# Split input weights kept in device memory for the later blocks, and another placing of the first Fourier transfers, in a hybrid encoder layer

## The chip, the cores and the metric

The kernel runs on one core of one Trainium2 chip. The metric is the device time of one execution in microseconds (us): the median of three runs of the kernel before is 3038.52 us (3036.92 to 3041.12). The engines are named as in the profile: PE multiplies matrices, with PEld for its weight loads; DVE works on vectors, ACT does activations, casts and copies, POOL does general vector work, and SP issues most of the DMA transfers. A transfer is issued by an engine in the order of that engine's program.

## The reference

One encoder layer over two sequences, 1024 tokens (prompt) and 2048 tokens (sample), model width 1024. Shortened:

```python
u = rms_norm(h, norm_w)
proj = u @ w_in
z_f, u_f, z_s, xbc, dt_raw = split(proj)
# Fourier group: 8 groups of 64 channels
four = fft2(u_f, axes=(seq, channel), norm='ortho').real
y_f = einsum(four, w_fmix) * silu(z_f)
# bidirectional state-space group: 24 heads of 64, 4 groups, state 128, chunks of 128
xbc = silu(conv5(xbc) + conv_b);  xs, Bm, Cm = split(xbc)
dt_f, dt_b = softplus(dt_raw + bias)
y_s = ssd_chunked(xs, dt_f, A_f, Bm, Cm) + flip(ssd_chunked(flip(xs), ...)) + D * xs
y_s = group_rms_norm(y_s * silu(z_s)) * ssd_norm_w
h = h + concat(y_f, y_s) @ w_out
h = h + (p @ w_ple_in) * sigmoid(h @ w_ple_gate)
out = rms_norm(h, final_norm_w)
```

Everything is float32. The matrix products keep nearly that precision by splitting each factor into a high part (the value rounded to the matmul's fp32r format) and a low part (the rest), with three products: high by high, high by low and low by high.

## The kernel before

**Stage 1** (0 to about 1977 us in the profile) does the normalization, the input projection and the whole state-space group. It runs over three blocks of about 1024 tokens: the prompt (block 0) and the two halves of the sample (blocks 1 and 2). The normalized rows of a block stay on the chip, transposed, as `uh` and `ul`, in three pieces of 342 tokens. The projection is cut into 40 *jobs* of 128 output columns each (C, B, x and z for the state-space group, uf and zf for the Fourier group) and a small one for dt. A job has three *pieces*, one for each 342 tokens: 24 matmuls into `ps` (L361), then a copy or a gate out of PSUM.

The weights of a job, 1024 by 128 values, come straight from `w_in` into the one buffer `wr` (`weights_in`, L179 to L183, issued by SP in L182). `weights_split` (L185 to L191) makes two tiles from them: ACT casts `wh<-wr` (L189), and POOL subtracts, `wl<-wr,wh` (L190). There are two buffers each of `wh` and `wl`. Each of the three blocks loads and splits all 40 jobs anew, which makes 120 of each.

Stage 1 has an order written out by hand. One slot is one piece, and `pre(slot, ...)` and `post(slot, ...)` put other work ahead of it or behind it; `step()` (L286) emits what is due. The list `rows_` (L729 to L743) names the jobs in their order: a first row with C, dt and B taken in turns piece by piece; uf 0; then x and z of each of the 12 units (a pair of heads), with the other jobs between; a last row with uf 3 and zf 3 in turns. The weights' times are set in L746 to L758:

```python
j.split_at = max(coming[m - 2].last + 1, k.split_at + 2)
pre(k.split_at + 1, j.load)
pre(j.split_at, j.split)
```

For a job in the steady rows this places the split three slots ahead of the job's first matmul, and the load two slots ahead of the split.

In the slots of each unit stands the state-space work: broadcast rows come back from device memory (`R<-ROWd` L540, `er<-EXPd` L635), POOL masks them (L548), ACT takes exponentials (L558), DVE joins them, PE multiplies (`pd` L575). POOL makes the weighted inputs `xw` (L587), from which PE makes the chunk states `pst` (L607); POOL also applies the gates (L658 to L663), and SP stores y (`Yd<-y`, L667). Of dt, `dt_turned`, `dt_softplus`, `dt_sums` (PE's `pcs` L469, then `acs` on ACT, L471) and `dt_rows` (PE's `prw`, L493) follow the first row at slots that are written down in L806 to L817. In the last row of a block the next block's x is loaded, normalized and turned (`x_in`, `x_norm`, `x_turn`; PE's `pt` L264, then `uh` L267 and `ul` L268). The conv's four outer taps are on DVE (L402).

**Stage 2** (about 1977 to 2101 us) is the Fourier group of both sequences, first the prompt's. It needs the block matrices `bd` and `wbd`, the stored projections U and the tables `traw`, all requested by SP (L900, L907, L913, L928). PE's first product here is `pm<-wbd,bd` (L972), and DVE folds U (`Ue<-U`, L982). **Stage 3** (to about 2700 us) is the output projection, in a scheme of seven products for a pair of chunks (L1102), and **stage 4** does the gated embedding and the final norm. In stages 2 to 4 a scheduler sets the order. Pools of SBUF grow from a left and a right side, so that a tile of a new stage can start when the tile that had its place is no longer read.

Of the kernel before, what the change touches and what calls it, by code (L numbers as in the profile page):

```python
# [18 lines left out]
P = 128  # L19
# [37 lines left out]
def tile_hybrid_encoder(ctx: ExitStack, tc: tile.TileContext, a):  # L57
# [20 lines left out]
    WSd = [dram.tile([P, 7, 4, 512], F32, name=f"WSd{i}") for i in range(3)]  # L78
    PLd = dram.tile([P, 2, DM], F32, name="PLd")
# [22 lines left out]
    with ExitStack() as ph:  # L102
# [76 lines left out]
        def weights_in(c0):  # L179

            raw = wp.tile([P, KT, P], F32, tag="wr", bufs=1, name="wr")
            nc.sync.dma_start(raw, w_in[:, c0:c0 + P].rearrange("(k p) c -> p k c", p=P))  # L182
            return raw  # L183

        def weights_split(raw):  # L185

            wh = wp.tile([P, KT, P], F32R, tag="wh", name="wh")
            wl = wp.tile([P, KT, P], F32R, tag="wl", name="wl")
            S.copy(wh, raw)  # L189
            G.tensor_tensor(wl, raw, wh.bitcast(F32), op=ALU.subtract)  # L190
            return wh, wl  # L191

# [43 lines left out]
        U = {}  # L236

# [74 lines left out]
        class Job:  # L312
# [64 lines left out]
            def end(self):  # L377
                B, k, i, s_ = self.B, self.kind, self.i, slot[0]
                if k == "C":
                    B.CT[i] = CT = gp.tile([P, TB], F32, tag="CT", name="CT")  # L380
                    conv(16 + i, self.dst, CT, s_ + (2 if i else 4))
# [348 lines left out]
        for bi, B in enumerate(blocks):  # L730
# [3 lines left out]
            rows_.append((B, [J("dt"), J("C"), J("B")] if bi else [J("C"), J("dt"), J("B")], "first"))  # L734
# [10 lines left out]

        n_, coming = 0, []  # L746
        for _, js, _ in rows_:
            for k, j in enumerate(js):
                j.last = n_ + 2 * len(js) + k
                if j.c0 is not None:  # L750
                    coming.append(j)
            n_ += 3 * len(js)
        coming[0].split_at = coming[1].split_at = -1
        for m in range(2, len(coming)):
            j, k = coming[m], coming[m - 1]
# [19 lines left out]
        with tc.manual_schedule():  # L775
# [23 lines left out]
            for i in range(3, 9):  # L799
                if i > 3:  # L800
                    pre(i - 4, x_norm, b0, i)
                if i > 5:
                    pre(i - 6, x_in, b0, i)
                post(i - 3, x_turn, b0, i)
# [76 lines left out]
    with ExitStack() as ph:  # L881
# [51 lines left out]
        for i in range(2):  # L933
            load_table(i, (0, 1))
# [451 lines left out]
```

## Time and profile before

| | us |
|---|---|
| median of three runs | 3038.52 |
| the profiled execution | 3031.59 |
| its span | 3029.8 |
| stage 1 | 0 to about 1977 |
| stage 2, Fourier group | 1977 to 2101 |
| stage 3, products | 2101 to 2700 |
| stage 4, outputs | 2700 to 3030 |

The profiled execution is 6.93 us under the median. The page gives for each engine the time in which it was busy; the windows give the same for a stretch of the span, with the granted clock of PE, the mean busy share of the DMA engines and the rate that they moved. A line of the waits reads "engine and its instruction <- who ended the wait: us in total, times, longest". A line of the timeline reads "start, duration, engine, line, operation, output<-inputs", with the idle time just before it and its releaser in brackets. A row with SPq is SP's DMA queue: the time it took to issue, waits included.

Two places of the profile outside the prediction's rows: in stage 3 PE is busy for 509.34 of 549.00 us (2101 to 2650), and in stage 4 for 320.97 of 329.80 us.

### The profile page before, as it was taken

The page shows a single profiled execution, that of the slowest core. Times are in us where ns is not written, and L with a number is a line of the kernel's source. Part 1 is how long each engine was busy: PE and PEld are TensorE (multiplying, and loading weights), DVE is VectorE, ACT ScalarE, POOL GpSimd, SP SyncE. Part 2 cuts the span into 40 slices and gives each one's busy share as a digit, 9 for nine tenths or more (in the row PEclk, how much of TensorE's full clock was granted, in tenths as well). Part 3 has the DMA queues.
Part 4 walks back from the last instruction along what each step waited for, and adds up shares of the span by engine and source line. Part 5 has one row for each costly group of instructions (what it writes and reads, how often), then busy time and mean ns, then how long its engine had stood idle before and what let it go on. Part 6 is the DMA issues. An engine that isn't in the chain of part 4 may idle for free. (4 is left out here: it accounts for less than half of the span.)

```text
span 3029.8 us, 47051 instructions
## 1 busy us (share of the span) xinstructions
PE 2836.0 (94%) x17252; PEld 2566.2 (85%) x17252; DVE 2228.9 (74%) x3412; ACT 1389.1 (46%) x2980; POOL 1475.5 (49%) x1114
## 2 busy tenths in 40 slices
PE   6899999989999899989999999969999899989998
PEld 6899989988999889989999999957677677768887
DVE  3687767666687568666779787687989988875665
ACT  4444545434544454434544444434433533354554
POOL 1355645431567565642555655455777578610000
PEclk9999999999999999999999999979999999999999
DMA  3378878972588778862677787566554644352221
GB/s 96 76 129 162 158 157 173 139 142 79 125 171 167 152 181 165 154 167 64 127 154 146 159 144 158 117 210 250 173 184 132 236 149 150 133 198 91 94 85 69
DMA packets 454579, 440.56 MB, mean 145 GB/s; under 512 B 24384, under 2 KB 405444, under 8 KB 450508
## 3 DMA queue, kind: packets, MB, share of 16 engines
q1 hardware_dynamic: 454060, 436.50, 60.6%
q8 instruction: 137, 2.24, 0.3%
q14 instruction: 94, 0.77, 0.1%
q10 hardware_dynamic: 288, 1.05, 0.1%
HBM read 328.41 MB, written 110.10 MB: 145 GB/s over the span
## 5 line engine op out<-in xcount | busy, mean ns | idle before, releaser
L361 PE MATMUL ps<-uh,wh 128*128 128x342 f32 (+1 forms) x2880 | 961.6, 334 | 8.4 <-ACT uh L267 8.4
L361 PE MATMUL ps<-ul,wh 128*128 128x342 f32 (+1 forms) x2880 | 926.3, 322 | 2.5 <-DVE ul L268 2.5
L361 PE MATMUL ps<-uh,wl 128*128 128x342 f32 (+1 forms) x2880 | 927.4, 322 | 0.4 <-POOL wl L190 0.4
L190 POOL TENSOR_TENSOR wl<-wr,wh 128x1024 fp32r<-128x1024 f32 x120 | 305.5, 2546 | 707.9 <-ACT wh L189 650.5
L361 PEld LDWEIGHTS ps<-uh,wh 128*128 128x128 f32 x2880 | 552.2, 192 | 20.1 <-ACT uh L267 9.2
L361 PEld LDWEIGHTS ps<-ul,wh 128*128 128x128 f32 x2880 | 554.5, 193 | 4.2 <-DVE ul L268 3.5
L361 PEld LDWEIGHTS ps<-uh,wl 128*128 128x128 f32 x2880 | 550.4, 191 | 1.2 <-POOL wl L190 1.1
L558 ACT ACTIVATE R<-R,lb 128x128 f32<-128x128 f32 x1152 | 356.8, 391 | 98.3 <-POOL R L548 98.2
L548 POOL TENSOR_SCALAR_AFFINE_SELECT R<-R 128x512 f32<-128x512 f32 x288 | 257.5, 905 | 193.7 <-DMA R<-ROWd 187.2
L618 DVE SCALAR_TENSOR_TENSOR H<-H,cd,pst 128x64 f32<-128x64 f32 x888 | 182.6, 274 | 47.7 <-PE pst L607 44.6
L402 DVE SCALAR_TENSOR_TENSOR xT<-raw,cvt,xT 128x1024 f32<-128x1024 f32 x144 | 214.8, 1492 | 2.6
L1102 PE MATMUL X<-whP,ah 128*128 128x512 f32 x480 | 195.2, 407 | 8.0 <-ACT pu L1111 6.4
L1102 PE MATMUL X<-wlP,ah 128*128 128x512 f32 x480 | 193.6, 403 | 1.6 <-DVE wlP L861 1.6
L1102 PE MATMUL X<-whP,al 128*128 128x512 f32 x480 | 192.5, 401 | 2.4 <-DVE al L1073 2.4
L587 POOL TENSOR_TENSOR xw<-xm,wd 128x512 f32<-128x512 f32 x144 | 181.8, 1268 | 18.7 <-PE pst L607 18.5
L367 ACT COPY raw<-ps 128x342 f32<-128x342 f32 x180 | 78.3, 438 | 241.7 <-PE ps L361 226.8
L1214 POOL TENSOR_TENSOR ht<-ht,pu 128x512 f32<-128x512 f32 x96 | 151.9, 1590 | 63.1 <-ACT pu L1111 43.0
L607 PE MATMUL pst<-xw,Bm 128*128 128x128 f32 x1056 | 151.3, 285 | 24.0 <-POOL xw L587 23.8
L607 PEld LDWEIGHTS pst<-xw,Bm 128*128 128x128 f32 x1056 | 131.9, 192 | 41.6 <-POOL xw L587 30.3
L189 ACT CAST wh<-wr 128x1024 fp32r<-128x1024 f32 x120 | 125.8, 1049 | 67.9 <-DMA wr<-in_w_in 67.2
L1073 DVE TENSOR_TENSOR al<-s,ah 128x512 fp32r<-128x512 f32 x144 | 143.6, 1021 | 16.4 <-ACT ah L1072 16.3
L563 DVE TENSOR_TENSOR R<-R,R 128x512 f32<-128x512 f32 x144 | 134.1, 931 | 25.9 <-ACT R L558 23.5
(264 smaller groups left out, 5703.9 us busy)
## 6 DMA issues: line engine op xcount, KB each, us to landing
R<-ROWd SPq DMA_DIRECT2D x288, 256.0 KB
wr<-in_w_in SPq DMA_DIRECT2D x120, 512.0 KB
er<-EXPd SPq DMA_DIRECT2D x288, 128.0 KB
Hd<-ht SPq DMA_DIRECT2D x48, 512.0 KB
ht<-Hd SPq DMA_DIRECT2D x48, 512.0 KB
y<-Yd SPq DMA_DIRECT2D x46, 512.0 KB
wlP<-WSd SPq DMA_DIRECT2D x21, 1024.0 KB
Yd<-y SPq DMA_DIRECT2D x72, 256.0 KB
```

The source lines that it names most:

```text
L190: G.tensor_tensor(wl, raw, wh.bitcast(F32), op=ALU.subtract)
L361: T.matmul(ps[:, :n], lhsT=wt[:, kt, :], rhs=ut[:, kt, :n], start=(i == 0), stop=(i == 3 * KT - 1))
L402: V.scalar_tensor_tensor(dst, raw[:, k:k + TB], cvt[:, 20 * k + ct:20 * k + ct + 1], dst, op0=ALU.mult, op1=ALU.add)
L548: G.affine_select(out=R.rearrange("p c h l -> p (c h) l"), in_=R.rearrange("p c h l -> p (c h) l"), pattern=[[0, 4], [sgn, P]], compare_op ...
L558: S.activation(R[:, c, h, :], R[:, c, h, :], AF.Exp, bias=self.B.lb[:, 2 * p + c, hc + h:hc + h + 1])
L563: V.tensor_tensor(E[0], E[0], E[1], op=ALU.add)
L587: G.tensor_tensor(xw, self.xm[c4].rearrange("p c (h e) -> p c h e", h=2), col(self.B.wd[:, c4:c4 + 4, hc:hc + 2]).broadcast_to([P, 4, 2, 6 ...
L607: T.matmul(pst[:, c, :], lhsT=B.Bm[self.g][:, c4 + c, :], rhs=xw[:, c, :, :].rearrange("p h e -> p (h e)"), start=True, stop=True)
L618: V.scalar_tensor_tensor(dst[:, e], H[d][:, cc, e], B.cd[:, cc, hc + h:hc + h + 1], pst[:, c, e], op0=ALU.mult, op1=ALU.add)
L1073: V.tensor_tensor(al, src, ah.bitcast(F32), op=ALU.subtract)
L1102: T.matmul(ps, lhsT=at[:, k, :], rhs=wt[:, k, :], start=(first and i == 0), stop=(i == 11), skip_group_check=not first)
L1214: return lambda t: G.tensor_tensor(h, h, t, op=ALU.add)
```

## The change

Four things change together.

1. In block 0 each job's `wh` and `wl` are stored, two slots after the split, to tiles `WPd` in device memory (two stores of 512 KB, 4 KB in a row for each partition). In blocks 1 and 2 a job loads both from there. POOL's subtraction is gone there; in its place ACT casts both tiles onto themselves, which makes them fp32r without a change of value.
2. The split comes one slot ahead of the job's first matmul, the load two slots ahead of that.
3. The first row of a block holds only C and dt, and B gets a row of its own; dt's steps come two to four slots earlier. The last row's pieces have another order, the next block's turns in it move by up to one slot (a few later, the last ones earlier), and the x of the kernel's start is handled earlier.
4. The pools of the Fourier stage change sides: its input tiles now lie over the normalized rows, which the last projection frees. Its first transfers (`bd`, `wbd`, the first two U, the first four table pieces) are issued by ACT instead of SP.

```diff
+    WPd = [[dram.tile([P, KT, P], F32, name=f"WPd{i}_{x}") for x in range(2)] for i in range(C_DT // P)]
...
             def load(self):
-                self.raw = weights_in(self.c0)
+                if self.B.bi == 0:
+                    self.raw = wp.tile([P, KT, P], F32, tag="wr", bufs=1, name="wr")
+                    nc.sync.dma_start(self.raw, w_in[:, self.c0:self.c0 + P].rearrange("(k p) c -> p k c", p=P))
+                else:
+                    self.w = self.places()
+                    for x, wt in enumerate(self.w):
+                        nc.sync.dma_start(flat(wt).bitcast(F32), flat(WPd[self.c0 // P][x]))
...
             def split(self):
-                self.w = weights_split(self.raw)
+                if self.B.bi == 0:
+                    self.w = wh, wl = self.places()
+                    S.copy(wh, self.raw)
+                    G.tensor_tensor(wl, self.raw, wh.bitcast(F32), op=ALU.subtract)
+                    for x, wt in enumerate(self.w):
+                        pre(slot[0] + 2, nc.sync.dma_start, flat(WPd[self.c0 // P][x]), flat(wt).bitcast(F32))
+                else:
+                    for wt in self.w:
+                        S.copy(flat(wt), flat(wt).bitcast(F32))
...
-            rows_.append((B, [J("dt"), J("C"), J("B")] if bi else [J("C"), J("dt"), J("B")], "first"))
+            rows_.append((B, [J("dt"), J("C")] if bi else [J("C"), J("dt")], "first"))
+            rows_.append((B, [J("B")], None))
...
+            if what == "last":
+                turn = [(0, 0), (0, 1), (1, 0), (0, 2), (1, 1), (1, 2)]
...
-            j.split_at = max(coming[m - 2].last + 1, k.split_at + 2)
-            pre(k.split_at + 1, j.load)
-            pre(j.split_at, j.split)
+            j.load_at = coming[m - 2].last + 1
+            pre(j.load_at, j.load)
+            pre(max(j.first - 1, j.load_at), j.split)
...
-                    post(q + 7, dt_turned, B)
-                    pre(q + 8, dt_softplus, B, 0)
-                    pre(q + 9, dt_softplus, B, 1)
-                    post(s0 + 13, dt_sums, B)
-                    post(s0 + 14, dt_rows, B)
-                    pre(s0 + 16, dt_out, B)
+                    post(q + 5, dt_turned, B)
+                    pre(q + 6, dt_softplus, B, 0)
+                    pre(q + 7, dt_softplus, B, 1)
+                    post(q + 10, dt_sums, B)
+                    post(q + 12, dt_rows, B)
+                    pre(q + 14, dt_out, B)
...
-                    for i, s_ in enumerate((2, 3, 4, 4, 5, 6, 8, 9, 10)):
-                        pre(s0 + (0, 0, 1, 2, 2, 3, 5, 6, 7)[i], x_in, b, i)
+                    for i, s_ in enumerate((3, 4, 5, 5, 6, 7, 7, 8, 9)):
+                        pre(s0 + (0, 0, 1, 2, 3, 4, 5, 6, 7)[i], x_in, b, i)
...
-        ft_ = ph.enter_context(tc.tile_pool(name="ft_", bufs=1, **R_))
-        fp = ph.enter_context(tc.tile_pool(name="fp", bufs=2, **R_))
-        fq = ph.enter_context(tc.tile_pool(name="fq", bufs=2, **L_))
-        fc = ph.enter_context(tc.tile_pool(name="fc", bufs=1, **L_))
+        ft_ = ph.enter_context(tc.tile_pool(name="ft_", bufs=1, **L_))
+        fp = ph.enter_context(tc.tile_pool(name="fp", bufs=2, **L_))
+        fc = ph.enter_context(tc.tile_pool(name="fc", bufs=1, **R_))
+        fq = ph.enter_context(tc.tile_pool(name="fq", bufs=2, **R_))
...
-        nc.sync.dma_start(bd, a["bdft"].rearrange("k p c -> p k c"))
+        nc.scalar.dma_start(bd, a["bdft"].rearrange("k p c -> p k c"))
...
-        first_u = [load_u(0, 0)]
+        first_u = [load_u(0, 0, nc.scalar)]
```

How this moves instructions is seen at three places. The first is the border between stage 1 and the Fourier stage. Before, SP's program held the first Fourier transfers behind the last stores of stage 1: ZFd and HBd are stage 1's results, y the last tokens of the state-space group.

```order
L979 DMA Z<-ZFd_65 128x1024
L288 DMA ZFd_66<-ft 128x1024
L288 DMA HBd<-hend 128x128
L667 DMA Yd_62<-y 128x512 x2
L900 DMA bd<-in_bdft 128x2x128
L913 DMA U<-UFd_63 128x1024
L907 DMA wbd<-in_w_fmix 64x4x64 x2
L928 DMA traw<-in_tabs 128x512 x2
```

In the changed kernel the same transfers stand in ACT's program, behind its last exponentials of the broadcast rows R (L567 is L558 before) and the last gate of a projection.

```order
L262 ACTIVATE ft<-ps 128x342
L567 ACTIVATE R_20712<-R_20712,lb 128x128 x4
L567 ACTIVATE R_20714<-R_20714,lb 128x128 x4
L920 DMA bd<-in_bdft 128x2x128
L927 DMA wbd<-in_w_fmix 64x4x64 x2
L933 DMA U<-UFd_63 128x1024
L948 DMA traw<-in_tabs 128x512 x2
L933 DMA U<-UFd_63 128x1024
L994 ACTIVATE mt<-pm 128x256
```

The transfers thus no longer follow the stores of y, and wbd now comes ahead of U.

The second place is SP's program in block 0, where the broadcast rows R and the raw weights wr of two following jobs are asked for. Before:

```order
L540 DMA R_2411<-ROWd_67 128x2x256
L540 DMA R_2413<-ROWd_67 128x2x256
L540 DMA R_2508<-ROWd_67 128x2x256
L540 DMA R_2510<-ROWd_67 128x2x256
L182 DMA wr<-in_w_in 128x8x128
L667 DMA Yd_60<-y 128x512
L540 DMA R_2632<-ROWd_67 128x2x256
L540 DMA R_2634<-ROWd_67 128x2x256
```

And in the changed kernel:

```order
L549 DMA R_1992<-ROWd_67 128x2x256
L549 DMA R_1994<-ROWd_67 128x2x256
L278 DMA WPd_0_100<-wh 128x1024
L278 DMA WPd_1_101<-wl 128x1024
L315 DMA wr<-in_w_in 128x8x128
L549 DMA R_2093<-ROWd_67 128x2x256
L549 DMA R_2095<-ROWd_67 128x2x256
L278 DMA WPd_0_80<-wh 128x1024
L278 DMA WPd_1_81<-wl 128x1024
L676 DMA Yd_60<-y 128x512
```

Two stores of 512 KB have come into SP's queue for every job, ahead of the next weights and rows.

The third place is POOL's program in block 1, around the weighted inputs xw that PE's chunk states need. Before:

```order
L548 AFFINE_SELECT R_8801<-R_8801 128x512
L548 AFFINE_SELECT R_8803<-R_8803 128x512
L587 TENSOR_TENSOR xw<-xm,wd 128x512
L190 TENSOR_TENSOR wl<-wr,wh 128x1024
L658 TENSOR_TENSOR y<-y,zT 128x512
L662 TENSOR_TENSOR er_8697<-er_8697,elt 128x512
L663 TENSOR_TENSOR zT<-er_8697,zT 128x512
L587 TENSOR_TENSOR xw<-xm,wd 128x512
```

And in the changed kernel:

```order
L557 AFFINE_SELECT R_8959<-R_8959 128x512
L557 AFFINE_SELECT R_8961<-R_8961 128x512
L596 TENSOR_TENSOR xw<-xm,wd 128x512
L667 TENSOR_TENSOR y<-y,zT 128x512
L671 TENSOR_TENSOR er_8853<-er_8853,elt 128x512
L672 TENSOR_TENSOR zT<-er_8853,zT 128x512
L596 TENSOR_TENSOR xw<-xm,wd 128x512
```

The subtraction of the weights between two xw is gone; the rest of the order here stands.

More of the change, by code (lines that the diff above doesn't have):

```diff
@@ L798, in tile_hybrid_encoder @@
             post(2, small_constants)
-            for i in range(3, 9):
+            for i, (n_in, n_norm, n_turn) in enumerate(
+                    ((0, 0, 0), (0, 0, 0), (0, 0, 1), (0, 1, 2), (1, 2, 2), (1, 2, 3)), 3):
+                if i > 5:
+                    pre(n_in, x_in, b0, i)
                 if i > 3:
[L801 to L804, printed above, removed]
-            pre(9, decay_rates)
-            for B, js, what in rows_:
+                    pre(n_norm, x_norm, b0, i)
+                post(n_turn, x_turn, b0, i)
+            pre(8, decay_rates)
+            for (B, js, what), row in zip(rows_, pieces):
                 bi, s0 = B.bi, slot[0]
@@ L830, in tile_hybrid_encoder @@
                             pre(s0 + 2 * i, norm_piece, BLOCKS[bi + 1], i)
-                for si in range(3):
-                    for j in js:
-                        step(lambda: j.piece(si))
+                for j, si in row:
+                    step(lambda: j.piece(si))
             while before or behind_:
@@ L1151, in tile_hybrid_encoder @@
     with ExitStack() as ph:
[L1152 removed]
+        yp = ph.enter_context(tc.tile_pool(name="yp", bufs=1, **L_))
         hbs, behind = [], []
```

77 lines of the change are left out of this document (38 added, 39 removed).

## The prediction

> **What bounds the kernel now.** The page's head and its busy times come first, to see which engine sets the length.
>
> ```profile
> span 3029.8 us, 47051 instructions
> PE 2836.0 (94%) x17252; PEld 2566.2 (85%) x17252; DVE 2228.9 (74%) x3412; ACT 1389.1 (46%) x2980; POOL 1475.5 (49%) x1114
> ```
>
> PE is busy for 2836.0 of 3029.8 us. No matmul is added or removed by the change, so what it can win is PE's idle time, 193.8 us over the whole span, and what it can lose are new waits of PE. Next, the windows by stage show where this idle time lies.
>
> ```profile
> core 0: us, PE busy (x) PEld busy (x) DVE busy (x) ACT busy (x) POOL busy (x), PEclk, DMA share, GB/s
> 0.00:120.00 120.00, 86.56 (x504) 81.86 (x505) 60.80 (x91) 53.69 (x94) 15.19 (x12) 0.93 0.27 77
> 120.00:630.00 510.00, 498.10 (x3494) 479.57 (x3493) 368.50 (x641) 253.66 (x588) 274.22 (x217) 0.99 0.82 150
> 630.00:760.00 130.00, 115.61 (x752) 110.66 (x751) 85.11 (x122) 51.92 (x102) 34.31 (x23) 0.92 0.45 102
> 760.00:1300.00 540.00, 510.67 (x3554) 489.96 (x3553) 386.96 (x665) 257.46 (x592) 330.29 (x258) 0.98 0.78 160
> 1300.00:1430.00 130.00, 116.25 (x754) 111.18 (x753) 85.76 (x124) 51.47 (x102) 46.73 (x31) 0.92 0.41 110
> 1430.00:1960.00 530.00, 524.64 (x3725) 506.04 (x3724) 406.70 (x692) 247.26 (x582) 286.07 (x229) 1.00 0.73 145
> 1960.00:2000.00 40.00, 19.45 (x135) 17.59 (x133) 23.65 (x63) 8.88 (x29) 11.99 (x11) 0.76 0.64 161
> 2000.00:2050.00 50.00, 43.65 (x208) 38.16 (x209) 48.22 (x105) 22.39 (x60) 30.89 (x18) 0.78 0.66 223
> 2650.00:2700.00 50.00, 40.34 (x164) 30.07 (x163) 35.09 (x44) 26.50 (x48) 14.90 (x10) 0.93 0.79 290
> ```
>
> PE's idle time in stage 1, from 0 to 2000 us, is 33.4, 11.9, 14.4, 29.3, 13.8, 5.4 and 20.6 us in the first seven of these rows, 128.8 in all. Of 193.8 us two thirds therefore lie where the change works. The third fact is who ended PE's waits:
>
> ```profile
> PE pst L607 <- POOL xw L587: 23.8, 18, 3.8
> PE pst L607 <- POOL xw L587: 22.0, 15, 3.8
> PE pt L264 <- DVE xt L250: 20.8, 5, 11.8
> PE prw L493 <- ACT acs L471: 17.2, 3, 7.6
> PE pm L972 <- DMA wbd<-in_w_fmix: 16.0, 1, 16.0
> PE pt L264 <- DVE H L618: 11.4, 4, 3.5
> PE ps L361 <- ACT uh L267: 8.4, 3, 6.4
> ```
>
> Columns are total, times and longest. The second row is the first one's share between 680 and 1960 us, nearly all of it. These rows name almost every place that the change touches, and they cap what it can win.
>
> **T1, the start of the Fourier stage.** Before, the small matrix wbd and the first U are requested by SP's queue.
>
> ```profile
> 1978.37 8.13 SPq L667 DMA_DIRECT2D Yd<-y  x2
> 1986.55 0.43 SPq L900 DMA_DIRECT2D bd<-in_bdft  x1
> 1987.07 0.46 SPq L913 DMA_DIRECT2D U<-UFd  x1
> 1967.35 2.43 ACT L558 ACTIVATE R<-R,lb 128x128 f32<-128x128 f32 x8
> 1966.65 0.31 PE L361 MATMUL ps<-uh,wl 128*128 128x342 f32 x1
> 1992.23 0.69 DVE L982 TENSOR_TENSOR Ue<-U 128x511 f32<-128x511 f32 x1 [3.87 <-DMA U<-UFd]
> ```
>
> SP sits on the last two stores of y for 8.13 us, since y isn't ready, and only then reaches U, at 1987.07; DVE uses U at 1992.23, 5.2 us later. In the new order ACT issues these transfers behind its last exponentials, which end at 1967.35 + 2.43 = 1969.8. With some 2 us for four issues U is asked for at about 1972 and there at 1977.5, 14.7 us earlier. The buffers are also freed by the last projection, at 1967.0, rather than by the tail of the state-space work. Not all of this reaches the end: from 2000 to 2050 DVE is busy for 48.2 of 50 us, so the start is bound by DVE, and what counts is the DVE idle time that gets used, 40 − 23.65 = 16.3 us between 1960 and 2000. The tail's DVE work, which ends near 1985, now runs among the Fourier folds. Bounds: −15, all the lead kept, and −2, if only the issue times (0.43 + 0.46 and about as much again for wbd) leave the path. I take **−13**, near the first, since SP's 8.13 us and PE's single wait of 16.0 us stand in one chain.
>
> The Trainium skill speaks against this term: "DMA: Bandwidth & Descriptors", section "Issuing engines are not separate DMA queues", says that transfers from several issuing engines share the same 16 DMA engines, so that using another engine saves only the time it takes to issue. By that alone T1 would be the −2; the 8.13 us that SP was held shows a second saving, the place in line.
>
> **T2, block 0 pays for the copies.** Each of the 40 jobs now stores its wh and wl, 512 KB each. No row shows such a store between projections. The highest rate among the windows shown is 290 GB/s at a DMA share of 0.79, 367 GB/s for full queues, so 1 MB costs 2.86 us of queue time, and 39 jobs in the block's steady part 112 us. The queues' free time in 120 to 630 us is 510 × 0.18 = 92 us. So the stores don't quite fit by this count, though they sit on no dependency path until block 1, and a share of 0.82 at only 150 GB/s says that much of the present occupancy is slow small packets, not bytes. What may get late are the row broadcasts that share SP's queue, and the raw weights, whose split now comes one slot before use, not three. A slot is one piece of 24 projection matmuls and the work placed beside it; 369 slots in 1977 us are 5.4 us each with the block changes in it, and I take 4.8 for the steady rows.
>
> ```profile
> L190 POOL TENSOR_TENSOR wl<-wr,wh 128x1024 fp32r<-128x1024 f32 x120 | 305.5, 2546 | 707.9 <-ACT wh L189 650.5
> L189 ACT CAST wh<-wr 128x1024 fp32r<-128x1024 f32 x120 | 125.8, 1049 | 67.9 <-DMA wr<-in_w_in 67.2
> 393.96 1.06 ACT L719 ACTIVATE xt<-xt 114x1024 f32<-114x1024 f32 x1 [9.14 <-DMA xt<-in_x_sample]
> ```
>
> The split takes 1.05 + 2.55 = 3.6 of these 4.8 us, so 1.2 us of cover is left; the last row shows ACT held 9.14 us by one late transfer of x, which costs nothing now and would cost about 8 then. Bounds: 0, if the queue absorbs all, and +40, about 1 us for each of 40 jobs. I take **+12**, nearer the lower end, ten jobs that come 1.2 us late, because PE lost just 11.9 us in this window under a share of 0.82.
>
> **T3, POOL without the subtraction in blocks 1 and 2.** 80 of the 120 subtractions at 2546 ns go, 204 us of POOL. This is one of the places where PE waited:
>
> ```profile
> 1019.45 2.39 POOL L190 TENSOR_TENSOR wl<-wr,wh 128x1024 fp32r<-128x1024 f32 x1 [0.70 <-ACT wh L189]
> 1021.79 1.28 POOL L658 TENSOR_TENSOR y<-y,zT 128x512 f32<-128x512 f32 x1
> 1023.03 1.05 POOL L662 TENSOR_TENSOR er<-er,elt 128x512 f32<-128x512 f32 x1
> 1024.16 1.26 POOL L663 TENSOR_TENSOR zT<-er,zT 128x512 f32<-128x512 f32 x1
> 1025.38 1.05 POOL L587 TENSOR_TENSOR xw<-xm,wd 128x512 f32<-128x512 f32 x1
> 1026.48 1.16 PE L607 MATMUL pst<-xw,Bm 128*128 128x128 f32 x8 [2.60 <-POOL xw L587]
> ```
>
> The xw behind the subtraction ends at 1026.4, and PE, which had stood for 2.60 us, starts then. Without 2.39 us of subtraction and the wait of 0.70 ahead of it, it ends 3.1 us earlier, which covers all but the longest of the 15 waits (mean 22.0 / 15 = 1.5, longest 3.8). Bounds −22 and −6, the latter if these waits come from late rows that POOL cuts. I take **−20**.
>
> **T4, just-in-time pairs in blocks 1 and 2.** Each job now loads 1 MB rather than 512 KB, 80 × 512 KB more, and ACT makes two casts in place (2.1 us) in the slot before use.
>
> ```profile
> ACT wh L189 <- DMA wr<-in_w_in: 54.5, 29, 4.9
> POOL R L548 <- DMA R<-ROWd: 187.2, 106, 5.0
> ```
>
> Between 680 and 1960 us ACT waited for the raw weights in 29 of some 76 jobs, 1.9 us in the mean, 4.9 at most, with three slots still ahead. The load is again two slots ahead of the cast, but the second half lands some 1.4 us (512 KB at 367 GB/s) later, and the cover is 4.8 − 2.1 = 2.7 us. So a job whose wait is above 2.7 − 1.4 = 1.3 us makes PE late, perhaps 20 of the 29, by some 0.6 us: **+12**. Bounds: 0, when the contiguous 4 KB of a partition move faster than the raw columns did, and +25, when the later loads also delay the row broadcasts of the second row shown and the copies out of PSUM behind the casts on ACT.
>
> **T5, the dt rows.** In the first rows dt's turn, softplus and sums come two to four slots earlier, and B leaves the interleaved row.
>
> ```profile
> PE pcs L469 <- DVE atm L446: 0.7, 1, 0.7
> L402 DVE SCALAR_TENSOR_TENSOR xT<-raw,cvt,xT 128x1024 f32<-128x1024 f32 x144 | 214.8, 1492 | 2.6
> ```
>
> The 17.2 us at prw become mostly covered, as two slots (9.6 us) rather than one now lie between the sums and the rows. On the other side the sums follow the softplus after three slots, and two taps of C's convolution on DVE (2 × 1.49 = 3.0 us) now lie inside that chain, so a wait of about 3 us per block can take the place of the 0.7 at pcs. −17 + 9 = **−8**, bounds −16 and +4.
>
> **T6, the kernel's start and the block changes.** ACT's uh (8.4), the xt of the turns (20.8, of which one wait of 11.8 at the very start stays) and H at the turns (11.4) add up to 28.8 us. The earlier x loads and the later turns address them; I take a third, **−10**, with bounds −20 and 0, since nothing in the rows says that the x loads themselves come sooner under a fuller queue.
>
> **T7, products and outputs.** Order of instructions is unchanged; 0, bounds ±3.
>
> **The sum** is −13 + 12 − 20 + 12 − 8 − 10 + 0 = −27 us. The profiled execution took 3031.59 us (span 3029.8 and 1.8 around it), so 3004.6; the median of the runs is 3038.52, 6.9 above it, which makes **3011**. About 0.2%, 6 us, is what a measurement of this kernel can tell from no change.
>
> **The rivals.**
>
> - A, the forecast: gains of 51, costs of 24. 2990 to 3030, chance 0.44.
> - C, the waits go and the costs stay hidden: T2 and T4 are 0, T5 −12, T6 −15, so −60 and 2978. For it: PE's small loss in block 0 under the fullest queue. Against it: one slot of cover. Chance 0.20.
> - B, slower: DMA becomes the bound of block 0. If only half of the 92 free us can be used, 112 − 46 = 66 us of the stores remain and PE waits for them, T2 = +66, sum +27, 3065. It decides as soon as T2 passes 39, that is, when less than 73 of the 92 us are usable. For it: broadcasts of 256 KB already make POOL wait 106 times. Against it: bytes at 150 GB/s are far below 367. Chance 0.18.
> - D, the xw waits hang on the row broadcasts and not on the subtraction: T3 is −6 and T5 0, sum −5, 3033, no change to be told. For it: POOL waited 187.2 us for these rows. Against it: the timeline at 1019 to 1026 us, with no wait for R in it. Chance 0.12.
> - E, the queue's name changes nothing: U's arrival is set by the shared DMA engines, still moving the last stores at a share of 0.64. T1 is −2, sum −16, 3022. Against it: the issue stood behind 8.13 us of waiting, not of moving. Chance 0.06. (This is the rule of the Trainium skill named at T1; no row of this case shows one queue beside another at the same place.)
>
> The range runs from 2965 to 3060: it takes in C with its spread below and the nearer part of B above. A's own range is 2990 to 3030. Faster: 0.42 of A, C, E and a little of D, 0.70; same: most of D and the edges, 0.12; slower: 0.18.
>
> **What would show it.** T1: pm's wait of 16.0 us falls below 5, and Ue stands near 1978 − 1967 = 11 us behind the last projection matmul. T2: DMA share above 0.9 in block 0, and PE waiting at the projection for POOL's wl or ACT's wh; without such waits C holds. T3: pst's waits for xw below 5 us in blocks 1 and 2. T4: ACT's casts waiting for transfers of WPd, and PE for these casts, some 12 us. T5: prw's waits gone, pcs's about 3 us per block. The forecast is wrong if block 0 gets longer by over 40 us, if xw's waits stay with POOL idle ahead of them, or if the later stages move by more than 5 us though their order stands.

## The result, and the profile after

The changed kernel takes 3147.28 us in the median of four runs (3142.01 to 3153.80), the kernel before 3038.43 beside it: a ratio of 1.0358 (95% interval 1.0333 to 1.0384), 109 us **slower**. The forecast was 3011 us with a range of 2965 to 3060. The page of the changed kernel, with the same head and two of its groups (columns as before):

```profile
span 3151.2 us, 47428 instructions
PE 2878.5 (91%) x17252; PEld 2597.3 (82%) x17252; DVE 2103.5 (67%) x3412; ACT 1467.8 (47%) x3060; POOL 1218.5 (39%) x1034
L370 PE MATMUL ps<-uh,wh 128*128 128x342 f32 (+1 forms) x2880 | 972.9, 338 | 76.5 <-ACT wh L334 45.7
L411 DVE SCALAR_TENSOR_TENSOR xT<-raw,cvt,xT 128x1024 f32<-128x1024 f32 x144 | 195.8, 1360 | 2.6
```

The span grew by 121.4 us with the same 17252 matmuls. PE is busy 42.5 us longer and idle 78.9 us longer: both have to be explained. The windows by stage, at the places shown of before:

```profile
core 0: us, PE busy (x) PEld busy (x) DVE busy (x) ACT busy (x) POOL busy (x), PEclk, DMA share, GB/s
120.00:630.00 510.00, 471.19 (x3196) 449.92 (x3194) 323.20 (x582) 235.52 (x540) 236.75 (x200) 0.96 0.83 199
760.00:1300.00 540.00, 501.72 (x3398) 480.76 (x3396) 333.24 (x606) 283.12 (x589) 204.79 (x201) 0.97 0.74 175
1430.00:1960.00 530.00, 499.46 (x3408) 478.74 (x3409) 337.32 (x624) 260.23 (x546) 154.30 (x165) 0.96 0.67 162
```

From 120 to 630 us the DMA share is 0.83, as it was (0.82), while the rate rose from 150 to 199 GB/s, and PE issued 3196 matmuls instead of 3494. The free share that the prediction counted on, 0.18, was not taken up. In the later blocks POOL is lighter, as planned, and PE does less all the same (3398 matmuls instead of 3554, 3408 instead of 3725). Who ended PE's waits (total, times, longest):

```profile
PE ps L370 <- ACT wh L334: 45.7, 19, 6.0
PE ps L370 <- POOL wl L329: 28.8, 18, 2.6
PE ps L370 <- ACT wh L328: 23.9, 10, 6.9
PE ps L370 <- ACT wl L334: 19.2, 24, 1.4
PE pt L254 <- DVE xt L240: 17.7, 4, 12.1
PE pt L254 <- DVE H L627: 15.7, 3, 7.3
PE pm L992 <- DMA wbd<-in_w_fmix: 10.9, 1, 10.9
PE ps L362 <- DVE ul L258: 10.1, 6, 4.2
PE pm L992 <- DVE ed L1022: 7.7, 1, 7.7
PE ps L370 <- ACT uh L257: 6.8, 3, 4.7
PE pst L616 <- POOL xw L596: 0.7, 1, 0.7
PE pcs L478 <- DVE atm L455: 0.3, 1, 0.3
```

The first four rows are new, but for 0.4 us of waits for wl before. The projection itself now waits for its weights, 117.6 us in all: 52.7 in block 0 (L328, L329) and 64.9 in blocks 1 and 2 (L334). What the change aimed at is gone: xw fell from 23.8 to 0.7, and prw's waits for acs (17.2) don't appear any more. That xw's waits went because POOL no longer subtracts is not shown by this; e2 below has another reason.

These waits cost more than their length. Short windows of PE around one of them, at 1062.8 to 1068.8 us:

```profile
core 0: us, PE busy (x), PEclk, DMA share, GB/s
1062.00:1064.00 2.00, 0.83 (x8) 1.00 0.53 114
1064.00:1066.00 2.00, 0.00 (x0) 1.00 0.95 234
1066.00:1068.00 2.00, 0.00 (x0) 1.00 1.01 190
1068.00:1070.00 2.00, 0.94 (x2) 0.53 1.02 195
1070.00:1072.00 2.00, 1.94 (x7) 0.50 1.09 112
1072.00:1074.00 2.00, 2.00 (x9) 0.50 0.91 248
1074.00:1076.00 2.00, 2.00 (x12) 0.76 1.03 347
1076.00:1078.00 2.00, 2.00 (x17) 1.00 1.11 96
```

After the wait PE's granted clock is about half for some 6 us. In that time a projection matmul starts about every 0.285 us, where one started every 0.16 us before the wait (the timeline from 1059.69 to 1074.79 us). Over the whole span the mean granted clock fell from 0.972 to 0.959. What is missing to full clock is 0.028 of 3029.8 us before, 85 us, and 0.041 of 3151.2 us after, 129 us; these 44 us more are enough to account for the 42.5 us by which PE is busy longer. The Trainium skill, "TensorE: Matmul & The Clock Gate", section "Part 1: The HAM clock gate (the "warmup" mystery)", says that PE falls to half clock after an idle window of about 3.4 us; the rows agree for this wait, with 0.50 after 6 us of it, and here the slow stretch lasts some 6 us. A shorter wait was enough too: one of 2.63 us, which ended at 1658.42 us, was followed by a clock of 0.50 from 1659 to 1662 us.

### The profile page after: what moved, and what is told of

It reads as the page before. It is cut to its first block, busy times and chain, and to the rows that moved or that the text cites. A ratio compares the mean times of both kernels' runs of the same rounds, so it can differ in the third digit from the quotient of the medians.

```text
span 3151.2 us, 47428 instructions
## 1 busy us (share of the span) xinstructions
PE 2878.5 (91%) x17252; PEld 2597.3 (82%) x17252; DVE 2103.5 (67%) x3412; ACT 1467.8 (47%) x3060; POOL 1218.5 (39%) x1034
## 2 busy tenths in 40 slices
DMA packets 405941, 524.46 MB, mean 166 GB/s; under 512 B 26944, under 2 KB 326084, under 8 KB 401868
## 5 line engine op out<-in xcount | busy, mean ns | idle before, releaser
L370 PE MATMUL ps<-uh,wh 128*128 128x342 f32 (+1 forms) x2880 | 972.9, 338 | 76.5 <-ACT wh L334 45.7
L370 PE MATMUL ps<-uh,wl 128*128 128x342 f32 (+1 forms) x2880 | 945.8, 328 | 48.0 <-POOL wl L329 28.8
L370 PE MATMUL ps<-ul,wh 128*128 128x342 f32 (+1 forms) x2880 | 938.3, 326 | 2.0 <-DVE ul L258 2.0
L370 PEld LDWEIGHTS ps<-uh,wl 128*128 128x128 f32 x2880 | 560.6, 195 | 63.1 <-POOL wl L329 35.2
L557 POOL TENSOR_SCALAR_AFFINE_SELECT R<-R 128x512 f32<-128x512 f32 x288 | 218.4, 764 | 809.7 <-DMA R<-ROWd 641.8
L567 ACT ACTIVATE R<-R,lb 128x128 f32<-128x128 f32 x1152 | 354.1, 392 | 35.6 <-POOL R L557 35.5
L329 POOL TENSOR_TENSOR wl<-wr,wh 128x1024 fp32r<-128x1024 f32 x40 | 100.2, 2504 | 353.4 <-ACT wh L328 315.2
L596 POOL TENSOR_TENSOR xw<-xm,wd 128x512 f32<-128x512 f32 x144 | 171.6, 1193 | 100.3 <-PE pst L616 83.5
L411 DVE SCALAR_TENSOR_TENSOR xT<-raw,cvt,xT 128x1024 f32<-128x1024 f32 x144 | 195.8, 1360 | 2.6
L263 DVE SCALAR_TENSOR_TENSOR zT<-zT,ps 128x342 f32<-128x342 f32 (+1 forms) x108 | 54.8, 508 | 170.5 <-ACT zT L262 169.7
L661 DVE TENSOR_TENSOR yt<-po,er 128x512 f32<-128x512 f32 (+1 forms) x144 | 91.2, 633 | 105.8 <-PE po L658 98.7
```

Source lines behind the costliest of these rows:

```text
L329: G.tensor_tensor(wl, self.raw, wh.bitcast(F32), op=ALU.subtract)
L370: T.matmul(ps[:, :n], lhsT=wt[:, kt, :], rhs=ut[:, kt, :n], start=(i == 0), stop=(i == 3 * KT - 1))
L411: V.scalar_tensor_tensor(dst, raw[:, k:k + TB], cvt[:, 20 * k + ct:20 * k + ct + 1], dst, op0=ALU.mult, op1=ALU.add)
L557: G.affine_select(out=R.rearrange("p c h l -> p (c h) l"), in_=R.rearrange("p c h l -> p (c h) l"), pattern=[[0, 4], [sgn, P]], compare_op ...
L567: S.activation(R[:, c, h, :], R[:, c, h, :], AF.Exp, bias=self.B.lb[:, 2 * p + c, hc + h:hc + h + 1])
L596: G.tensor_tensor(xw, self.xm[c4].rearrange("p c (h e) -> p c h e", h=2), col(self.B.wd[:, c4:c4 + 4, hc:hc + 2]).broadcast_to([P, 4, 2, 6 ...
```

## The experiments

The table gives medians and ratios to the kernel before on the same chip, and from each profile the length of blocks 0, 1 and 2 (first projection matmul of a block to that of the next) and the time from the last projection matmul to the end of the span. Kernels that ran on different chips are compared by their ratios; 0.01 is 30 us. A block's length comes from one profile and varies: block 1 has the same program in before, e4, e5, e6, e8 and e11, and took 669 to 683 us.

| kernel | median us | ratio (95%) | blocks 0 / 1 / 2, us | rest, us |
|---|---|---|---|---|
| before | 3038.43 | | 659 / 669 / 618 | 1063 |
| changed | 3147.28 | 1.0358 (1.0333 to 1.0384) | 699 / 697 / 663 | 1071 |
| e1 | 3149.37 | 1.0351 (1.0318 to 1.0383) | 713 / 691 / 655 | 1072 |
| e2 | 3058.66 | 1.0056 (1.0039 to 1.0074) | 644 / 676 / 644 | 1071 |
| e3 | 3033.20 | 0.9972 (0.9953 to 0.9991) | 651 / 665 / 625 | 1068 |
| e4 | 3104.90 | 1.0200 (1.0169 to 1.0231) | 723 / 683 / 613 | 1063 |
| e5 | 3073.03 | 1.0109 (1.0074 to 1.0144) | 690 / 673 / 614 | 1069 |
| e6 | 3063.87 | 1.0062 (1.0037 to 1.0088) | 683 / 673 / 622 | 1064 |
| e7 | 3136.04 | 1.0300 (1.0272 to 1.0328) | 697 / 691 / 645 | 1071 |
| e8 | 3040.42 | 0.9994 (0.9981 to 1.0008) | 659 / 672 / 612 | 1069 |
| e9 | 3032.65 | 0.9975 (0.9959 to 0.9992) | 653 / 669 / 623 | 1071 |
| e10 | 3024.46 | 0.9950 (0.9934 to 0.9966) | 654 / 663 / 617 | 1072 |
| e11 | 3054.39 | 1.0046 (1.0026 to 1.0066) | 666 / 676 / 615 | 1062 |
| e12 | 3020.10 | 0.9942 (0.9921 to 0.9964) | 648 / 659 / 617 | 1069 |
| e13 | 3077.96 | 1.0118 (1.0091 to 1.0145) | 703 / 655 / 628 | 1072 |
| e14 | 3050.02 | 1.0031 (1.0020 to 1.0042) | 700 / 636 / 625 | 1076 |

The first question was whether the weights come late because load and split stand too near to their use, or because of the added traffic.

**e1: block 0 with the old lead, stores kept.**

```diff
+            if j.B.bi == 0:
+                j.split_at = max(coming[m - 2].last + 1, k.split_at + 2)
+                pre(k.split_at + 1, j.load)
+                pre(j.split_at, j.split)
```

> The changed kernel, but in block 0 the raw weights are loaded and split at the slots of the kernel before (split three slots ahead of use); the stores stay, and blocks 1 and 2 stay. Theory L (lead: the weights come late because load and split stand too near to their use): PE's waits for wh and wl in block 0 (23.9 + 28.8 us) fall below 10 us and the clock lost behind them comes back, block 0 shortens from 699 to about 645 to 660 us, total about 3090 to 3105. Theory D (traffic: the stores fill the DMA queues, so that everything in block 0 is late): block 0 stays above 685 us, total about 3135 to 3150.

3149.37 us: nothing gained, block 0 at 713 us. The waits for weights in block 0 are gone, but PE waits for xw (29.3 us) and others instead. e3 below has the same block 0 without the stores and takes 651 us for it, 62 us less. In block 0 lead is not the cause.

**e2: the raw weights in all blocks, no stores, the changed kernel's late split.**

```diff
-                if self.B.bi == 0:
+                if True:
                     self.raw = wp.tile(...)
...
-                    for x, wt in enumerate(self.w):
-                        pre(slot[0] + 2, nc.sync.dma_start, flat(WPd[...][x]), flat(wt).bitcast(F32))
```

> The changed kernel without stores and without the kept copies: every block loads the raw weights and splits them on ACT and POOL, but at the changed kernel's slots (split one slot ahead). Theory L: all three blocks wait as block 0 does now, about 50 us of waits for wh and wl in each, and POOL's xw waits come back in blocks 1 and 2; total about 3130 to 3180. Theory D: with the traffic of the kernel before the waits fall below 15 us per block; total about 3030 to 3060.

3058.66: 92 us of the changed kernel's time, by the ratios, go with the traffic. Theory D has the total, but not the waits: 63.3 us of waits for weights remain (37.4 for wl, 25.9 for wh), 46.0 of them in blocks 1 and 2, which stay 10 and 19 us longer than in e3. PE's wait for xw in blocks 1 and 2 (665 to 1985 us) is now this:

```profile
PE pst L614 <- POOL xw L594: 0.9, 1, 0.9
```

In e3, with the old lead, it is 26.2 us. POOL makes all its subtractions in both, so with the later split xw's waits go though the subtraction stays, and waits for weights come in their place.

**e3: as e2, with the old lead as well** (its split times are the three lines of the kernel before).

> As e2, but load and split stand at the slots of the kernel before in all blocks; what is left of the change are the first and last rows, dt's steps and the Fourier stage. Both theories: no waits for wh and wl, prw's waits for acs (17.2 us) gone, xw's waits as before (about 22 us). Theory L and D: about 3015 to 3035. If it is above 3045, the rows or the Fourier stage cost time by themselves.

3033.20, as expected: the rows, dt's steps and the Fourier stage together are worth some 9 us (ratio 0.9972, so 3 to 14 us). The late split costs 25 us (e2 less e3), all of it in blocks 1 and 2.

**e4: the kernel before with nothing but the stores.**

```diff
                 self.w = weights_split(self.raw)
+                if self.B.bi == 0:
+                    for x, wt in enumerate(self.w):
+                        pre(slot[0] + 2, nc.sync.dma_start, WPd[...][x], wt)
```

> The kernel before with one thing added: block 0 stores wh and wl of each job to device memory, two slots after the split, as the changed kernel does (nothing reads them). Theory L: the stores cost 0 to 12 us, total 3038 to 3050. Theory D: block 0 grows by 30 us or more, total above 3068.

61 us more, with nothing that reads the copies. Over block 0, first the kernel before, then e4:

```profile
21.00:680.00 659.00, 619.95 (x4234) 595.66 (x4235) 452.69 (x764) 314.13 (x706) 305.74 (x238) 0.97 0.72 136
```

```profile
21.00:744.00 723.00, 631.24 (x4234) 604.88 (x4235) 454.81 (x763) 315.54 (x706) 294.19 (x238) 0.94 0.77 182
```

The rate rises from 136 to 182 GB/s, the share only from 0.72 to 0.77, and the block takes 64 us more. The stores bring 42 MB. The way to PE shows in the waits of the same two stretches, POOL's for the broadcast rows in before and in e4, and PE's for xw in e4:

```profile
POOL R L548 <- DMA R<-ROWd: 55.8, 35, 3.1
POOL R L553 <- DMA R<-ROWd: 122.5, 55, 5.4
PE pst L612 <- POOL xw L592: 33.9, 18, 4.6
```

The rows come later, POOL waits 67 us longer for them, and PE waits 33.9 us for POOL's xw, where it waited 1.8 in before. For wh and wl, with the old lead, PE's projection waits only 5.0 us (60 to 760 us).

**e5, e6 and e11: what of a store costs?** e5 issues the stores from ACT, e6 stores wh alone, e11 stores an eighth of each tile. The lines are shortened.

```diff
-                        pre(slot[0] + 2, nc.sync.dma_start, WPd[...][x], wt)
+                        pre(slot[0] + 2, nc.scalar.dma_start, WPd[...][x], wt)            # e5
+                        pre(slot[0] + 2, nc.sync.dma_start, WPd[...][0], wh)              # e6
+                        pre(slot[0] + 2, nc.sync.dma_start, WPd[...][x][:, :P], wt[:, :P])  # e11
```

> The kernel before plus the stores of block 0, issued by ACT instead of SP; slots as in e4. Theory O (occupancy: the stores take time of the DMA engines that block 0 does not have free, whoever issues them): as e4, 3090 to 3115. Theory Q (the place in SP's queue: rows and weights stand behind the stores and behind their waits): most of e4's 61 us goes, 3038 to 3060.

> The kernel before plus the store of wh alone, from SP: half the bytes and half the DMAs of e4, and no store that waits for POOL's wl. Theory O: half of the DMA time of e4's stores, of which the queues can absorb some 20 us, so 20 to 31 us over the kernel before, 3060 to 3072. Theory Q in its form that the wait for wl holds SP: 3038 to 3048.

> As e4 (the kernel before with stores in block 0 from SP), with the same number of stores at the same places, but each stores only the first of eight column tiles, 64 KB instead of 512 KB. Theory O (bytes): e4's cost of 61 us goes almost wholly, 3038 to 3050. Theory Q (each store's place and wait in SP's program, whatever its size): 3070 to 3105.

e6 has half of the bytes and costs 19 us by its ratio, a third of e4's 61, which is Theory O with some of the transfer absorbed: the second half of the stores costs more than the first. e11 makes as many stores as e4, and its trace has as many packets (466100), with 36.7 MB less (80 × 448 KB). It costs 14 us by its ratio; its 3054.39 us lie just above Theory O's range. So of e4's 61 us some 47 hang on bytes, 1.3 us for a MB in the mean (the intervals reach 9 us to either side of e4's cost, 6 of e11's). e5 lies between both expectations, at 33 us. How long the issues of the stores held their engine, first e4 on SP, then e5 on ACT (min/median/max ns):

```profile
L289 SPq DMA_DIRECT2D WPd<-wh x40: 337/934/4090, 36.0 to 717.9; - x40
L289 SPq DMA_DIRECT2D WPd<-wl x40: 325/594/3059, 36.4 to 719.7; - x40
```

```profile
L289 ACTq DMA_DIRECT2D WPd<-wh x40: 326/326/762, 35.8 to 677.2; - x40
L289 ACTq DMA_DIRECT2D WPd<-wl x40: 326/327/2311, 36.2 to 680.1; - x40
```

On SP a store held the engine that also issues every row and weight for 0.6 to 0.9 us in the median, up to 4.1; on ACT for 0.33. So bytes are the larger part, the place in SP's program another. But e11's small stores held SP about as long as e4's large ones (medians 0.59 and 0.75 us, up to 3.4), and e11 costs 14 us in all. Holding SP therefore hardly explains the 28 us that e5 saves against e4; what large stores in SP's queue do to the rows and weights behind them was not measured apart, and stays open.

**e7: in blocks 1 and 2 the high part with the old lead, the low part as changed.**

```diff
+                    self.raw = wp.tile([P, KT, P], F32, tag="wr", bufs=1, name="wr")
+                    nc.sync.dma_start(flat(self.raw), flat(WPd[self.c0 // P][0]))
...
+                pre(j.load_at, j.load_low)
+                pre(max(j.first - 1, j.load_at), j.split_low)
+                j.load_at = k.split_at + 1
+                j.split_at = max(coming[m - 2].last + 1, k.split_at + 2)
```

> The changed kernel, but in blocks 1 and 2 wh lands in the raw buffer, which is free there, and is asked for and cast at the slots of the kernel before (cast three slots ahead); only wl still lands in place. Stores and block 0 stay as in the changed kernel, and as many bytes move. Theory L for blocks 1 and 2 (they lose by lead, not by bytes): PE's waits for wh there (45.7 us) fall below 10, those for wl to below 25, the two blocks shorten by 25 to 45 us together, total 3100 to 3122. Theory O for them: the blocks stay as long, 3138 to 3152.

18 us less than the changed kernel by the ratios, and between the two expectations. PE's waits in e7, from 720 to 1410 us and from 1410 to 2075:

```profile
PE ps L375 <- ACT wl L328: 38.9, 11, 7.4
PE ps L375 <- ACT wl L328: 17.1, 9, 4.0
```

No wait for wh is left; the wait moved to wl, from 19.2 to 56.0 us. Lead helps the part that gets it, and the other part waits instead.

**e13 and e14: the changed kernel's lead and its number of loads, fewer bytes in blocks 1 and 2.**

```diff
-                        nc.sync.dma_start(flat(wt).bitcast(F32), flat(WPd[self.c0 // P][x]))
+                        n = P if x else KT * P       # e14: n = P for both
+                        nc.sync.dma_start(flat(wt)[:, :n].bitcast(F32), flat(WPd[self.c0 // P][x])[:, :n])
```

> The changed kernel, but in blocks 1 and 2 the load of wl brings only the first of eight column tiles (64 KB instead of 512 KB) and ACT spreads it over the others, so wl is not the right one there; the loads stand at the same slots and are as many, and 1.05 us of cast becomes about 1.2. Theory B (bytes): the weights come some 1.4 us earlier and the rows behind them too; blocks 1 and 2 come down to about those of e2 (676 and 644 us), total 3100 to 3118. Theory L (the lead alone, whatever is loaded): the blocks stay, 3138 to 3152.

> As e13, with both loads cut to 64 KB, so that wh and wl are wrong in blocks 1 and 2. Theory B: hardly any wait for weights is left there, and with POOL free of the subtraction the blocks come to about 650 and 610 us, total 3045 to 3075. Theory L: waits for the casts remain above 40 us, total above 3120.

73 and 99 us below the changed kernel by the ratios, with the lead untouched and as many packets (405941, in e13 one more). e13 lies under the range of Theory B. PE's waits for weights from 735 to 2000 us in e14:

```profile
PE ps L371 <- ACT wh L334: 8.8, 3, 3.2
PE ps L371 <- ACT wl L334: 1.1, 3, 0.6
```

64.9 us of waits have become 9.9. Bytes decide: 99 us for 73.4 MB left out (160 × 448 KB), 1.35 us for a MB in the mean, near the price in block 0. The mean hides that the price rises: of the two equal parts, the first that comes back (e14 to e13) costs 26 us, the second (e13 to the changed kernel) 73 us, 0.7 and 2.0 us for a MB. The first part is wh and the second wl, so how much is loaded and which part it is were not held apart; in block 0 the price rises in the same way, 19 us for the stores of wh (e6) and 42 more for those of wl (e4). e13 loads 576 KB for a job, little more than the 512 KB of the kernel before, and its blocks 1 and 2 take 1283 us together, where those of e3 take 1290. Lead is what the late bytes then run out of.

**e8: the Fourier stage alone, on the kernel before.**

> The kernel before with the Fourier stage of the changed kernel (pools on the other side, first transfers issued by ACT) and nothing else. The forecast's T1: 13 us from the last projection to the first product of the output stage, total about 3025. Theory H (the tail of the state-space work now stands on PE and DVE behind the first Fourier instructions, which wait for the same transfers, so the gap is moved and not filled): the stretch from the last projection to the first product stays 139 to 146 us, total 3036 to 3046.

No difference (0.9994, interval 0.9981 to 1.0008). Theory H holds. PE's waits in e8 between 1960 and 2110 us:

```profile
PE pm L972 <- DMA wbd<-in_w_fmix: 11.6, 1, 11.6
PE pm L972 <- DVE ed L1002: 11.2, 3, 8.8
```

The one wait of 16.0 us became two of 11.6 and 11.2 (the latter in three parts). Of the kernel before, SP's issue of wbd and PE's first product:

```profile
1987.62 1.28 SPq L907 DMA_DIRECT2D wbd<-in_w_fmix  x2
1992.83 1.19 PE L972 MATMUL pm<-wbd,bd 128*128 128x128 f32 x4 [16.03 <-DMA wbd<-in_w_fmix]
```

The changed kernel's own timeline shows why:

```profile
2079.87 0.31 PE L370 MATMUL ps<-uh,wl 128*128 128x342 f32 x1
2080.57 2.43 ACT L567 ACTIVATE R<-R,lb 128x128 f32<-128x128 f32 x8
2083.56 3.00 ACTq L920 DMA_DIRECT2D bd<-in_bdft  x1
2086.66 4.06 ACTq L927 DMA_DIRECT2D wbd<-in_w_fmix  x2
2091.75 0.35 ACTq L933 DMA_DIRECT2D U<-UFd  x1
2096.17 1.20 PE L992 MATMUL pm<-wbd,bd 128*128 128x128 f32 x4 [10.89 <-DMA wbd<-in_w_fmix]
2097.15 3.62 PE L658 MATMUL po<-CT,H 128*128 128x128 f32 x16
2097.75 0.69 DVE L1002 TENSOR_TENSOR Ue<-U 128x511 f32<-128x511 f32 x1 [11.25 <-DMA U<-UFd]
2098.48 1.63 DVE L573 TENSOR_TENSOR R<-R,cb 128x512 f32<-128x512 f32 x1
2113.74 1.22 PE L992 MATMUL pm<-wbd,bd 128*128 128x128 f32 x4 [7.69 <-DVE ed L1022]
```

Two things. ACT's issues of bd and wbd took 3.00 and 4.06 us, waits included, where SP's had taken 0.43 and 1.28, so U was asked for 8.7 us after ACT's last exponential and not 2. In e8 they took 0.45 and 4.42 us, and U was asked for 8.3 us after; why the issues take so long from ACT is not shown. And the rest of the state-space work (po on PE, R on DVE) stands behind pm and Ue in the order of their engines and waits with them; before, it ran while the transfers were on their way. pm comes 16.0 us after the end of the last projection matmul instead of 25.9, but DVE's last y of the tail ends 39.3 us after it instead of 17.9. The way to the first output product is no shorter: 140.0 us before, 142.3 in e8 and 145.1 in the changed kernel.

**e9, e10, e12: is there a better version?** All start from e3. e9 splits late in block 0 only, where e2 had the shortest one; e10 gives the subtraction of blocks 1 and 2 to DVE; e12 does both.

```diff
-                    G.tensor_tensor(wl, self.raw, wh.bitcast(F32), op=ALU.subtract)
+                    (V if self.B.bi else G).tensor_tensor(wl, self.raw, wh.bitcast(F32), op=ALU.subtract)
```

> As e3 (no copies; first and last rows and the Fourier stage of the change), but in block 0 the raw weights are split one slot ahead of use as in e2; blocks 1 and 2 keep the early split. If the late split costs by lead alone, block 0 gets no shorter than e3's 651 us and the total is 3033 to 3042. If in block 0 a late split helps (e2's block 0 was 644 us), by keeping the subtraction out of the way of xw or the raw loads out of the way of the rows, the total is 3022 to 3030.

> As e3, but in blocks 1 and 2 DVE makes the low part wl instead of POOL: T3's gain without any copy in device memory. Forecast by T3: PE's waits for xw there (21.1 + 5.1 us) fall below 5 us, 15 to 25 us less than e3, total 3008 to 3020. Rival: DVE, which then does 80 subtractions of 1 to 1.5 us more behind ACT's cast, is late with what PE waits for next (H, R), and the total stays within 5 us of e3, 3028 to 3038.

> e9 and e10 together: late split in block 0, wl by DVE in blocks 1 and 2. If both gains are there and add up: 3003 to 3014. If only one is: as the better of e9 and e10, within 5 us.

e9 is e3 again (3032.65): without the stores a late split in block 0 neither costs nor helps. Block 0 has the same program in e2, e9 and e12, and took 644, 653 and 648 us, so e2's 644 lies within the spread. e10 gains 9 us on e3, less than forecast and between its two expectations: xw's waits fall from 26.2 to 9.2 us (e3 from 660 to 1340 us and from 1340 to 1985, then e10 from 680 to 1960), but not to nothing.

```profile
PE pst L614 <- POOL xw L594: 21.1, 11, 3.5
PE pst L614 <- POOL xw L594: 5.1, 5, 1.9
```

```profile
PE pst L614 <- POOL xw L594: 9.2, 6, 2.4
```

e12, at 3020.10 us and a ratio of 0.9942 (0.9921 to 0.9964), is faster than both kernels, 18 us under before; it can't be told apart from e10. e12 and e9 ran on one chip and differ only in who subtracts in blocks 1 and 2: xw's waits there fall from 25.4 to 7.9 us, and the time by 10 us by the ratios. So about half of the 20 us of T3 is to be had without a byte more of traffic.

## Why the prediction was wrong

- **T2** (+12, bounds 0 and +40) failed. Measured alone it is +61 (e4). The step that failed is "nearer the lower end ... because PE lost just 11.9 us in this window under a share of 0.82". That little was lost showed only that PE didn't depend on the queues yet, not that the remaining 0.18 could be filled: the share went to 0.83 in the changed kernel, and the block grew. T2 named the row broadcasts too, but priced only late weights; in e4 the time went through the rows, POOL and xw (33.9 us). Rival B had the mechanism, the price (66) and the point of decision (39); it was given 0.18. That its price is so near has some luck in it: it counts bytes alone, and 14 of the 61 us stay when the stores shrink to an eighth (e11).
- **T4** (+12, bounds 0 and +25) failed by more. Its working counted only the delay of each job's second half, 1.4 us, against 2.7 us of cover. It left out that 42 MB more in the same queues put off every transfer, the first half too: PE waited 45.7 us for wh, the first half, and 19.2 for wl; in e13, where only wl's bytes are missing, the waits for wh are 22.4 us. The last 36.7 of these 42 MB cost 73 us (the changed kernel less e13). The late split was not the cost by itself: with nearly the old bytes, blocks 1 and 2 are no longer in e13 than in e3. The 25 us of e2 over e3 are those of another split, in which POOL's subtraction stands behind ACT's cast. The bounds were drawn from the lateness seen at the old traffic.
- **T3** (−20): 22.0 us of xw waits in blocks 1 and 2 became 0.7, but the changed kernel doesn't show that the subtraction was the cause, since in e2, where POOL still subtracts, they became 0.9. The mechanism is shown by e12 against e9, where DVE subtracts: 17.5 of 25.4 us of waits go, for 10 us of time.
- **T1** (−13) was wrong: 0 (e8). The lead was 10 us for pm and 8 for Ue instead of the 15 counted, and the tail's work, which the prediction saw "among the Fourier folds", stood behind the first of them. The order rows had shown this place on ACT, but not the place of po and R. The rule of the Trainium skill named at T1 ("DMA: Bandwidth & Descriptors", section "Issuing engines are not separate DMA queues"), by which the term was −2, came nearer. Its remark that the issue time, which is all that another issuing engine saves, is usually small beside the transfer did not foretell block 0, where the stores cost 61 us from SP (e4) and 33 from ACT (e5).
- **T5** (−8): prw's 17.2 us went, and pcs, for which 9 us were set against it, waited 0.3. **T6** (−10): the three rows of 40.6 us stand at 40.2 (6.8 + 17.7 + 15.7), and PE waits 10.1 us more for ul at dt; in e3, without the traffic, they stand at 42.4. The earlier x loads and later turns took nothing off these waits. T1, T5 and T6 together were −31; e3, which holds them all, gives −9.
- **T7** (0) was right, at the edge of its bounds of ±3: from the first output product to PE's end 914.3 us before and 917.5 after.
- **The clock** was no term at all. 42.5 of the 121.4 us by which the span grew are PE's longer busy time, and the lower granted clock is enough to account for them. Windows with a PEclk of 0.92 or less around the old waits stood in the prediction's own rows.

Put together from the runs: −9 (e3) + 61 (e4) − 7 (blocks 1 and 2 with the new split and nearly the old bytes, e13 less e3) + 73 (the other bytes there, the changed kernel less e13) = +118, where 109 was measured. Each term has an uncertainty of some 5 to 15 us, and the −7 comes from single profiles; so the sum is a consistency, not a proof of each term.

## What to carry to other kernels

Price a transfer that is added to a stretch by what the stretch pays for bytes, expect that price to rise as the stretch fills up, and treat a DMA share near 0.8 as full until a run shows otherwise: recomputing 80 subtractions, on POOL (e3) or on DVE (e10), was cheaper here than storing and reloading their results. Before costing a wait as hidden, count the traffic that the change itself adds to it, and add to each wait of PE the slow clock behind it. When first work of a new stage is moved forward, look at what comes to stand behind it on every in-order engine.

## What the runs showed of the hardware

- A PE wait of 6 us was followed by about 6 us at half the granted clock, so its cost is its length and some 2.5 us more (20 matmuls that start every 0.285 us instead of every 0.16). A wait of 2.63 us was followed by half the clock too (at 1658.42 us).
- One added MB cost about 1.3 us in the mean in two different stretches, as stores (e11 against e4) and as loads (e14 against the changed kernel), with as many packets in both kernels of each pair. The price rose as more was loaded: 0.7 us for a MB from e14 to e13, 2.0 from e13 to the changed kernel.
- The issue of a store took 0.33 us in the median on ACT (e5) and 0.59 to 0.93 us on SP in block 0, with up to 4.1 (e4), waits included. Cut to an eighth of their size, the stores held SP about as long (e11). ACT needed 4.06 us for two transfers of wbd at the end of stage 1.
- DVE's tap of 128 by 1024 is slower while POOL makes the subtractions. In e10, where DVE makes them in blocks 1 and 2, it took 1304 ns in the mean in block 1, and 1547 in e3; in block 0, where POOL subtracts in both, 1529 in both.
